# Context tokens' value sums on VectorE instead of TensorE, and a second PSUM buffer for the experts' first products

## The chip, the cores and the metric

The kernel runs on one core of a Trainium2 chip. The core has five engines with instruction queues of their own: TensorE (matrix products into PSUM), VectorE and ScalarE (element-wise work), GpSimd (here mostly the issue of gathers from memory) and SyncE (the issue of the other transfers). In the profile they are PE, DVE, ACT, POOL and SP. The metric is the device time of one execution in microseconds. Each engine works through its instructions in the order of the program and waits at an instruction until its operands and its output buffer are free.

## What is computed

A two-layer network over 512 latent tokens and 256 context tokens of width 1024: layer 0 is a gated DeltaNet, layer 1 attention, each followed by a mixer of experts (PEER). The mixer is what the change touches. For every token and each of 8 heads it picks 16 of 16384 experts by their scores; an expert is a row of the table u and a row of the table v:

```python
def block_fn(xb):
    ...
    idx = jnp.take_along_axis(cand_i, pos, axis=-1)          # 8 heads x 16 picks a token
    gate = jax.nn.softmax(best_s, axis=-1)
    act = jax.nn.gelu(jnp.einsum('pd,phkd->phk', xb, u_tab[idx]).astype(jnp.float32), approximate=False)
    coef = (gate * act).astype(xb.dtype)
    return jnp.einsum('phk,phkd->pd', coef, v_tab[idx])
```

The last line is the sum in question: for a token, 128 rows of v, each times a coefficient. Context tokens need the mixer in layer 0 only, since after layer 1's attention has read them nothing else does.

## The kernel before

Tokens are worked on in blocks of 128: latents 0 to 3, context 0 and 1. A mixer's tokens go one of two ways. Latents 0 to 2 (ND = 3) are evaluated *densely*: all 16384 experts in 128 blocks of 128, with a matrix of gates that is zero where an expert was not picked. Latent block 3 and, in layer 0, both context blocks are *gathered*: only the picked rows of u and v are read, with indirect transfers that GpSimd issues, 128 rows of 4 KB (one tile `row`) each.

In layer 0 the stages around the change follow one another like this: the DeltaNet; `routing` of the latents (the score products `qp` and the best 16 of each half, then the picks by block); `gates_build` (for each token two one-hot tiles A and B on VectorE and their product `gp` on TensorE); `dense` (for each of 128 blocks of experts the first products `up`, a Gelu into `c`, times the gates, and the second products `y` with the rows of v); then `attention`, which begins with a norm of each latent block and the projections `pa`. `act` computes `up` and the Gelu of one block; about half of the blocks are computed ahead, during `routing` and `gates_build` (`tock`), and their `c` is kept in memory. `up` has one PSUM bank, `y` has six.

The gathers are a background queue (`bg`) of generators. At fixed places in the loops `tick` adds a number from the table RATE to a credit and takes one step of the first generator for each whole credit; `drain(keep)` takes all steps at once until `keep` generators are left. A step issues one gather into one of four buffers `row` (GB = 4) and the instruction that uses it:

- `gather_u`: a scalar_tensor_tensor on VectorE that multiplies the rows by the tokens' values and sums along the row (L967).
- `gather_vt`, for latent block 3: partition t holds token t, step k gathers the k-th pick of all 128 tokens, and one scalar_tensor_tensor on VectorE (L984) adds row times coefficient to `y`; for block 3 the profile names this `lhs`.
- `gather_v`, for the context: a step gathers the 128 picks of one token. The sum over picks is a product on TensorE, `yp` (L1020): two calls of 512 columns, each with a 128x32 tile of `Cz` whose only nonzero column holds the token's coefficients. A call becomes two records in the trace. It works by halves of 64 tokens.

Three of the four context halves (NVA = 3) are queued ahead of the latents' gathers, the fourth behind them; it is left in the queue by `drain(2 * NX - NVA)` and taken within the attention's projections by their ticks and by the `drain()` ahead of the context's own norm, which reads its result. The order in which the attention takes latent blocks is 3, 1, 2, 0.

The instruction order on each engine is not the order in which the code is written. A scheduler (`schedule_with_timeline_sim=True`) reorders instructions while it builds the program; gathers and the VectorE instructions that use them keep their order among each other. Once built, the order is fixed.

Of the kernel before, what the change touches and what calls it, by code (L numbers as in the profile page):

```python
# [18 lines left out]
P = 128  # L19
# [12 lines left out]
AHEAD = [i for r in (0, 2, 1, 3) for i in range(r, PK, 4)]      # blocks of experts, in the order of their evaluation ahead  # L32


class Kern:
# [18 lines left out]
    # gathers are issued in small steps between the other work  # L54
# [67 lines left out]
    def ada(self, l, r, pool=None):  # L122
        """chunks 2 * r and 2 * r + 1 of a layer's modulations, for latents (row 0) and context (row 1)"""
# [24 lines left out]
    def mod_rows(self, pool, l, s, sub, norm, nb=1, pool_g=None, **kw):  # L148
        """A = norm_g*(1+scale), S = shift, as rows on all partitions"""
        nc = self.nc  # L150
        A = pool.tile([P, D], F32, name="modA", bufs=nb)
        S = pool.tile([P, D], F32, name="modS", bufs=nb)
        g = (pool_g or pool).tile([P, D], F32, name="modg", **kw)
        nc.sync.dma_start(g, self.I[norm][l:l + 1, :].to_broadcast([P, D]))
        self.ada_row(S, l, s, 3 * sub)
        self.ada_row(A, l, s, 3 * sub + 1)
        nc.vector.scalar_tensor_tensor(A, A, 1.0, g, op0=ALU.add, op1=ALU.mult)
        return A, S

    def norm_mod(self, pool, x, A, S, h):  # L160
        """h <- rmsnorm(x) * A + S"""
# [8 lines left out]
    def transp_split(self, pp, tag, h, hi, lo, b):  # L170
        """h [128, 1024] -> hi/lo[:, kb, b*128:...]"""
# [10 lines left out]
    # tokens on the free axis: 0..511 latents, 512..767 context  # L182
    def gate_math(self, p, pp, gx, n, G):
# [23 lines left out]
        # log1p(e) = ln(u) * e / (u - 1), or e where u rounds to 1  # L207
# [30 lines left out]
    def dn_in(self, G, later, ast, rec):  # L238
        """q, k, v, z and the gates; rec's first step is traced before the last heads, beside which it runs"""
# [67 lines left out]
    def dn_qkv(self, G, p, pp, pwp, hi, lo, wtile, heads, nb):  # L307
# [4 lines left out]
        W2 = TL + 4 + TC          # conv output span: latents, gap of 4, context  # L312
        XC = TL + 6               # start of the context in the padded row
# [83 lines left out]
    def dn_z(self, p, pp):  # L397
        """2 * silu(z)^T of the latents"""
# [24 lines left out]
    def dn_rec(self, seq, G, og_d, st_d):  # L423
# [5 lines left out]
        with ExitStack() as st:  # L429
# [8 lines left out]
            for g0 in range(0, QH, GR):  # L438
                pks, Pss, Us = [], [], []
                pg = p if g0 // GR % 2 else pq  # L440
                for hh in range(GR):
                    h = g0 + hh
                    Ps = pg.tile([P, MH, 2, P], F32, name="Pm", bufs=GR)
                    U = pg.tile([P, MH, 2, P], F32, name="U", bufs=GR)     # (c, v), dir
# [5 lines left out]
                    for c in range(n):  # L450
# [4 lines left out]
                        km = pq.tile([P, 2, 2, P], F32, name="km", bufs=2)     # (kk, kq), dir  # L455
                        nc.vector.tensor_mul(km, kk.unsqueeze(2).to_broadcast([P, 2, 2, P]), self.tri.unsqueeze(1).to_broadcast([P, 2, 2, P]))
                        rp = pqp.tile([P, 2, 2, P], F32, name="rp")
                        ar = pq.tile([P, 2, 2, P], F32, name="ar", bufs=2)     # (v, dir)
# [116 lines left out]
    def dn_inv(self, p, pp, Us, MH, Z64):  # L575
        """Us[head][:, m, dir] <- (I + U)^-1, U triangular (upper for dir 0, lower for dir 1)."""
# [23 lines left out]
        R1 = t4("R1", [P, 2 * M, 32])     # rows of the inverses' transposes  # L600
        R2 = t4("R2", [P, 2 * M, 32])     # rows of the inverses
# [9 lines left out]
        # (source, target) blocks  # L611
# [56 lines left out]
    def dn_out(self, seq, og_d, xin, xout, put):  # L668
        """xout[b] = xin[b] + g1 * (o @ w_out); put(b, rows) for every finished block"""
# [33 lines left out]
    def attention(self, xl, xc, order, rows, A0, gst, ost, pst):  # L703
        """(softmax(q k^T) v)^T of the latents, split, by heads; context is read after the gathers that finish it"""
# [134 lines left out]
    def attention_out(self, xl, xout, put):  # L839
        """xout[b] = xl[b] + g1 * (o @ w_out); put(b, rows) for every finished block"""  # L840
# [21 lines left out]
    def routing(self, l, hi, lo, T, gate, idx, order, done=None):  # L862
        """gate[b], idx[b]: [128 tokens, 8 heads, 16]"""
        nc, I = self.nc, self.I
        n = T // P
        with self.tc.tile_pool(name="rt", bufs=1) as q, self.tc.tile_pool(name="rtp", bufs=1, space=PS) as pp:
# [32 lines left out]
            for b in order:  # L899
# [29 lines left out]
                # places are STEP apart, so that the picked candidate's is the smallest difference  # L929
                nc.vector.tensor_add(ci, ci, iota.unsqueeze(1).to_broadcast([P, PH, NC_]))  # L930
                # the first eight picks lie in the staircase of eight
# [25 lines left out]
    def gather_u(self, l, p, hs, gate, idx, coef):  # L957
        """coef[t, (head, pick)] = gate * gelu(<u_pick, h_t>)"""
# [14 lines left out]
    def gather_vt(self, p, y, coef, idx, g2row, xin, put):  # L973
        """put(xin + g2 * sum over picks of coef * v_pick), by 128 tokens"""
# [20 lines left out]
    def gather_v(self, p, pv, pp, Cz, coef, idx, g2row, xin, xout, s):  # L995
        """xout = xin + g2 * sum over picks of coef * v_pick, by 64 tokens: partitions are (32 tokens, half row, token)"""
        nc = self.nc
        sl = lambda q: slice(32 * q, 32 * q + 32)
        hv = lambda q: slice(512 * (q % 2), 512 * (q % 2) + 512)
        l, r, m = g2row  # L1000
        ixf = pv.tile([P, P], F32, name="ixf")
        nc.vector.tensor_copy(ixf, idx.rearrange("p h k -> p (h k)"))
        yp = pp.tile([P, 512], F32, name="yp")
        nc.tensor.transpose(yp[:, 0:P], coef, self.ident)
        nc.tensor.transpose(yp[:, P:2 * P], ixf, self.ident)
        iT = pv.tile([P, P], I32, name="iT")
        nc.vector.tensor_copy(iT, yp[:, P:2 * P])
        cT = pv.tile([P, P], F32, name="cT")
        nc.vector.tensor_copy(cT, yp[:, 0:P])
        Cd = Cz.rearrange("p (g q) -> p g q", g=2)[:, :, 0:32 * 32:33]  # L1010
        nc.vector.tensor_copy(Cd, cT[:, 64 * s:64 * s + 64].rearrange("p (g i) -> p g i", g=2))
        yp = pp.tile([P, 512], F32, name="yp")
        for i in range(32):
            for g in range(2):
                t = 64 * s + 32 * g + i
                v = p.tile([P, D], F32, name="row", tag="row", bufs=self.gbufs)
                nc.gpsimd.indirect_dma_start(out=v, out_offset=None, in_=self.I["peer_v"],  # L1017
                                             in_offset=bass.IndirectOffsetOnAxis(ap=iT[:, t:t + 1], axis=0))
                for j in range(2):
                    nc.tensor.matmul(yp[sl(2 * g + j), :], Cz[:, (32 * g + i) * 32:(32 * g + i + 1) * 32], v[:, j * 512:(j + 1) * 512],  # L1020
                                     start=i == 0, stop=i == 31)
                if (i, g) == (28, 0):
                    fin = p.tile([P, D], F32, name="row", tag="row", bufs=self.gbufs)
                    xt, yt = fin[:, 0:512], fin[:, 512:D]
                    for q in range(4):
                        nc.sync.dma_start(xt[sl(q)], xin[64 * s + 32 * (q // 2):64 * s + 32 * (q // 2) + 32, hv(q)])
                        c0 = (m % 2) * D + 512 * (q % 2)
                        nc.sync.dma_start(yt[sl(q)], self.ada_d[l][m // 2][r:r + 1, c0:c0 + 512].to_broadcast([32, 512]))
                yield
        nc.vector.tensor_mul(yt, yt, yp)  # L1030
        nc.vector.tensor_add(yt, yt, xt)
        for q in range(4):
            nc.sync.dma_start(xout[64 * s + 32 * (q // 2):64 * s + 32 * (q // 2) + 32, hv(q)], yt[sl(q)])

    def gates_build(self, l, tbs, gate, idx, G_d, pk):
        """G_d[64-token group][j, i, t]: gate of expert i * 128 + j for every token; the last group is returned, in SBUF"""
# [201 lines left out]
def body(ctx, tc, I, out, dbg=None, upto=99):  # L1238
# [74 lines left out]
    for i in range(NVA):  # L1313
        vctx(i // 2, i % 2)
# [128 lines left out]
```

## Time and profile before

| | |
|---|---|
| time, median of three runs | 4883.66 us (4878.91 to 4895.90) |
| span of the profiled execution | 4891.1 us |
| TensorE busy | 4329.9 us, 89% |
| VectorE busy | 3587.0 us, 73% |
| ScalarE busy | 1866.5 us, 38% |
| GpSimd busy | 1321.5 us, 27% |
| memory traffic | 245 GB/s on average |

The profiled execution has no device time beside its span; the span is 7.4 us above the median and within the three runs. A row of a group reads: line of the code, engine, operation, output<-inputs, shapes, count, then busy time and mean length of one, then the idle time of the engine just ahead of these instructions and what ended it. In a row of stages the first figures are start and end in microseconds from the span's start. TensorE's records of successive products overlap, since they are pipelined; the distance of their starts is what one costs. VectorE's overlap a little as well.

### The profile page before, as it was taken

What the parts mean: (1) busy time and instruction counts of PE and PEld (TensorE: products, weight loads), DVE (VectorE), ACT (ScalarE), POOL (GpSimd) and SP (SyncE); (2) the same over time, 40 slices, a digit from 0 to 9 for tenths busy, and PEclk for the clock granted to TensorE, in tenths of its full rate; (3) what the DMA queues carried; (4) which work ended last, traced back from release to release, by engine and by line L of the source; (5) the groups of instructions that cost most, each with busy time, mean ns of one, the idle gap of its engine ahead of it and who ended that gap; (6) DMA issues with size and microseconds to landing.
All of it is one profiled execution on the core that took longest, in us unless ns stands there. A gap on an engine that the chain in (4) does not pass through costs nothing. (4 is left out here: it accounts for less than half of the span.)

```text
span 4891.1 us, 68996 instructions
## 1 busy us (share of the span) xinstructions
PE 4329.9 (89%) x24564; PEld 3455.1 (71%) x24564; DVE 3587.0 (73%) x8483; ACT 1866.5 (38%) x3605; POOL 1321.5 (27%) x1111
## 2 busy tenths in 40 slices
PE   6999669757569698999999999988997999999998
PEld 3778547545444556666788888745687998888887
DVE  4667825899965857566688888645579888888886
ACT  2335553447450213344333333223333554333333
POOL 0000000134344433222333334440000102444441
PEclk8999789768679899999999999999999999999999
DMA  7744246447578877777999999872133678999996
GB/s 296 261 150 135 75 144 191 153 148 254 177 242 317 301 240 268 269 260 272 329 349 351 339 339 337 292 268 74 61 112 107 215 260 287 355 334 335 336 324 230
DMA packets 480616, 1196.55 MB, mean 245 GB/s; under 512 B 40752, under 2 KB 239152, under 8 KB 470416
## 3 DMA queue, kind: packets, MB, share of 16 engines
q1 hardware_dynamic: 332816, 655.21, 38.2%
q0 software_dynamic: 147456, 536.94, 31.5%
q8 instruction: 194, 3.18, 0.3%
q14 instruction: 150, 1.23, 0.1%
HBM read 1079.50 MB, written 112.49 MB: 244 GB/s over the span
## 5 line engine op out<-in xcount | busy, mean ns | idle before, releaser
L965 POOL DMA_INDIRECT row<-in_peer_u,idx x512 | 613.2, 1198 | 1513.3 <-DVE row L967 706.3
L100 PE MATMUL up<-hil,uh 128*128 128x384 f32 x2048 | 709.4, 346 | 44.7 <-ACT c L1094 44.1
L102 PE MATMUL up<-hil,ul 128*128 128x384 f32 x2048 | 697.2, 340 | 0.0
L101 PE MATMUL up<-lol,uh 128*128 128x384 f32 x2048 | 696.1, 340 | 0.0
L100 PE MATMUL y<-vh,ch 128*128 128x512 f32 x1536 | 602.8, 393 | 9.1 <-ACT ch L106 7.6
L101 PE MATMUL y<-vl,ch 128*128 128x512 f32 x1536 | 602.9, 393 | 0.0
L102 PE MATMUL y<-vh,cl 128*128 128x512 f32 x1536 | 508.8, 391 | 0.0
L981 POOL DMA_INDIRECT row<-in_peer_v,idx x256 | 339.9, 1328 | 456.3 <-DVE lhs L984 374.5
L100 PEld LDWEIGHTS up<-hil,uh 128*128 128x128 f32 x2048 | 386.9, 189 | 94.8 <-ACT c L1094 65.4
L106 ACT CAST uh<-ur 128x1024 fp32r<-128x1024 f32 x256 | 268.3, 1048 | 454.3 <-PE up L101 322.3
L1017 POOL DMA_INDIRECT row<-in_peer_v,iT x256 | 279.5, 1092 | 557.7 <-PE yp L1020 473.7
L107 DVE TENSOR_TENSOR vl<-vr,vh 128x1024 fp32r<-128x1024 f32 x256 | 312.9, 1224 | 127.1 <-ACT vh L106 125.1
L106 ACT CAST vh<-vr 128x1024 fp32r<-128x1024 f32 x256 | 268.6, 1051 | 359.9 <-PE y L102 325.0
L101 PEld LDWEIGHTS up<-lol,uh 128*128 128x128 f32 x2048 | 387.1, 189 | 19.2 <-issue 10.9
L102 PEld LDWEIGHTS up<-hil,ul 128*128 128x128 f32 x2048 | 386.5, 189 | 18.2 <-issue 15.1
L107 DVE TENSOR_TENSOR ul<-ur,uh 128x1024 fp32r<-128x1024 f32 x256 | 312.1, 1220 | 74.7 <-ACT uh L106 70.1
L967 DVE SCALAR_TENSOR_TENSOR row<-row,ghs 128x1024 f32<-128x1024 f32 x256 | 311.2, 1222 | 73.7 <-DMA row<-in_peer_u,idx 72.7
L1066 DVE TENSOR_SCALAR A<-iotar,kt 128x128 f32<-128x128 f32 x768 | 221.8, 289 | 174.4 <-PE gp L1068 171.9
L100 PEld LDWEIGHTS y<-vh,ch 128*128 128x128 f32 x1536 | 289.8, 189 | 70.3 <-ACT ch L106 9.1
L102 PEld LDWEIGHTS y<-vh,cl 128*128 128x128 f32 x1536 | 288.6, 188 | 64.6 <-issue 4.2
L984 DVE SCALAR_TENSOR_TENSOR lhs<-row,lcf,lhs 128x1024 f32<-128x1024 f32 x254 | 325.1, 1280 | 9.6 <-DMA row<-in_peer_v,idx 8.0
L101 PEld LDWEIGHTS y<-vl,ch 128*128 128x128 f32 x1536 | 290.1, 189 | 56.3 <-issue 2.5
(397 smaller groups left out, 8788.1 us busy)
## 6 DMA issues: line engine op xcount, KB each, us to landing
ur<-in_uT SPq DMA_DIRECT2D x256, 512.0 KB
vr<-in_peer_v SPq DMA_DIRECT2D x256, 512.0 KB
w<-in_ada_w SPq DMA_DIRECT2D x48, 1024.0 KB
G_d<-st SPq DMA_DIRECT2D x10, 4096.0 KB
gt<-G_d SPq DMA_DIRECT2D x64, 640.0 KB
act_d<-c SPq DMA_DIRECT2D x129, 192.0 KB
c<-act_d SPq DMA_DIRECT2D x129, 192.0 KB
wr<-in_dn_w_in SPq DMA_DIRECT2D x48, 512.0 KB
```

Of the source, the lines that this page charges most:

```text
L100: first = mm(ps, lh, rh, start=start, stop=False)
L101: mm(ps, lh, rl, start=False, stop=False)
L102: mm(ps, ll, rh, start=False, stop=stop)
L106: self.nc.scalar.copy(hi, src)
L107: self.nc.vector.tensor_sub(lo, src, hi)
L965: nc.gpsimd.indirect_dma_start(out=u, out_offset=None, in_=self.I["peer_u"], in_offset=bass.IndirectOffsetOnAxis(ap=ix[:, k:k + 1], axis=0))
L967: mv = nc.vector.scalar_tensor_tensor(u, u, 1.0, hs, op0=ALU.mult, op1=ALU.mult, accum_out=coef[:, k:k + 1])
L981: nc.gpsimd.indirect_dma_start(out=v, out_offset=None, in_=self.I["peer_v"], in_offset=bass.IndirectOffsetOnAxis(ap=ix[:, k:k + 1], axis=0))
L984: keep(nc.vector.scalar_tensor_tensor(y, v, coef[:, k:k + 1], y, op0=ALU.mult, op1=ALU.add))
L1017: nc.gpsimd.indirect_dma_start(out=v, out_offset=None, in_=self.I["peer_v"], in_offset=bass.IndirectOffsetOnAxis(ap=iT[:, t:t + 1], axis=0))
L1066: nc.vector.tensor_scalar(A, iota, kt[:, 0, t:t + 1], None, op0=ALU.is_equal)
```

## The change

Both context blocks now use `gather_vt` like latent block 3: 128 steps a block, each a gather of one pick of 128 tokens and a multiply-add on VectorE into the block's own tile `ghs`. `gather_v`, its tables `Cz`, index transposes and PSUM bank are gone. The two context blocks are queued ahead of everything else, and `drain()` ahead of the attention empties the queue. The PSUM bank that came free becomes a second buffer of `up`, in both layers. Three numbers of layer 0's RATE differ: steps per score product in `routing` 5 to 3, per head in the picks 3 to 2.5, per group of four tokens in `gates_build` 0.88 to 1.2. The file also loses its comments; line numbers from 996 on are 40 lower.

```diff
-    def gather_v(self, p, pv, pp, Cz, coef, idx, g2row, xin, xout, s):
...
-        for i in range(32):
-            for g in range(2):
-                t = 64 * s + 32 * g + i
-                v = p.tile([P, D], F32, name="row", tag="row", bufs=self.gbufs)
-                nc.gpsimd.indirect_dma_start(out=v, out_offset=None, in_=self.I["peer_v"],
-                                             in_offset=bass.IndirectOffsetOnAxis(ap=iT[:, t:t + 1], axis=0))
-                for j in range(2):
-                    nc.tensor.matmul(yp[sl(2 * g + j), :], Cz[:, (32 * g + i) * 32:(32 * g + i + 1) * 32], v[:, j * 512:(j + 1) * 512],
-                                     start=i == 0, stop=i == 31)
...
-        ps = self.upp.tile([P, 512], F32, name="up")[:, :T]
+        ps = self.upp.tile([P, 512], F32, name="up", bufs=2)[:, :T]
...
-RATE = ([1.0, 3.3, 5.0, 3.0, 0.88, 2.6, 3.15, 2.6, 0.6, 3, 0.08], [0, 0, 0, 0, 0.27, 2.6, 0, 1.32, 6.25, 0, 0])
+RATE = ([1.0, 3.3, 3.0, 2.5, 1.2, 2.6, 3.15, 2.6, 0.6, 3, 0.08], [0, 0, 0, 0, 0.27, 2.6, 0, 1.32, 6.25, 0, 0])
...
-    gat.open_v(gst)
     k.dense_open(lst, 0, ND, hi, lo)
-    vctx = lambda b, s: gat.v_half(b, idx[1, b], (0, 1, 5), rows(xm_c, b), rows(xo_c, b), s)
-    for i in range(NVA):
-        vctx(i // 2, i % 2)
+    for b in range(NX):
+        gat.v(b, idx[1, b], (0, 1, 5), rows(xm_c, b), lambda y, b=b: nc.sync.dma_start(rows(xo_c, b), y))
...
-    for i in range(NVA, 2 * NX):
-        vctx(i // 2, i % 2)
...
-    k.drain(2 * NX - NVA)
+    k.drain()
```

What the scheduler makes of it is seen in the order of the instructions. First GpSimd's queue of gathers in layer 0, as the difference from before (idx_91 and idx_92 are the context blocks' picks, idx_90 latent block 3's):

```order
-L965 DMA row<-in_peer_u,idx_92 128x1024 x27
-L1017 DMA row<-in_peer_v,iT 128x1024 x192
+L965 DMA row<-in_peer_u,idx_92 128x1024 x29
+L981 DMA row<-in_peer_v,idx_91 128x1024 x128
+L981 DMA row<-in_peer_v,idx_92 128x1024 x128
 L965 DMA row<-in_peer_u,idx_90 128x1024 x128
 L981 DMA row<-in_peer_v,idx_90 128x1024 x128
-L1017 DMA row<-in_peer_v,iT 128x1024 x22
```

The gathers of the fourth half, of which the first 22 stand here, moved from behind the latents' gathers to ahead of them; the number of gathers is the same.

Second, VectorE near the start of `gates_build` of layer 0, before:

```order
L1066 TENSOR_SCALAR A<-iotar,kt 128x128
L1067 TENSOR_SCALAR B<-iotar,kt 128x128
L107 TENSOR_TENSOR ul<-ur,uh 128x1024
L1066 TENSOR_SCALAR A<-iotar,kt 128x128
L1067 TENSOR_SCALAR B<-iotar,kt 128x128
```

and now (`ghs` is a context block's sum):

```order
L1026 TENSOR_SCALAR A<-iotar,kt 128x128
L984 SCALAR_TENSOR_TENSOR ghs_6340<-row,gcf_6341,ghs_6340 128x1024
L1027 TENSOR_SCALAR B<-iotar,kt 128x128
L107 TENSOR_TENSOR ul<-ur,uh 128x1024
L1026 TENSOR_SCALAR A<-iotar,kt 128x128
L984 SCALAR_TENSOR_TENSOR ghs_6340<-row,gcf_6341,ghs_6340 128x1024
L1027 TENSOR_SCALAR B<-iotar,kt 128x128
```

The multiply-adds of gathered tiles stand between the one-hot tiles, where there were none.

Third, VectorE from the end of `dense` of layer 0 to the first norm of the attention, before (`rt_` is a finished block of the dense tokens, `hrow` the first tile of the attention):

```order
L1156 TENSOR_TENSOR rt__27332<-rt__27332,rx 128x512
L1155 TENSOR_TENSOR rt__27340<-y_20100,dg_27328 128x512
L1156 TENSOR_TENSOR rt__27340<-rt__27340,rx 128x512 x2
L88 TENSOR_SCALAR nm_ss<-nm_ss 128x1
L1155 TENSOR_TENSOR rt__27348<-y_20101,dg_27328 128x512
L1155 TENSOR_TENSOR rt__27348<-y_20102,dg_27328 128x512
L88 TENSOR_SCALAR nm_ss<-nm_ss 128x1
L1156 TENSOR_TENSOR rt__27348<-rt__27348,rx 128x512 x2
L166 SCALAR_TENSOR_TENSOR hrow<-lhs_12955,nm_ss,modA 128x1024
L166 SCALAR_TENSOR_TENSOR hrow<-rt__27340,nm_ss,modA 128x1024
```

and now:

```order
L1115 TENSOR_TENSOR rt__26994<-y_19786,dg_26974 128x512
L1116 TENSOR_TENSOR rt__26994<-rt__26994,rx 128x512 x2
L984 SCALAR_TENSOR_TENSOR lhs_12955<-row,lcf_12956,lhs_12955 128x1024 x2
L157 SCALAR_TENSOR_TENSOR modA<-modA,modg 128x1024
L984 SCALAR_TENSOR_TENSOR lhs_12955<-row,lcf_12956,lhs_12955 128x1024 x95
L991 TENSOR_TENSOR lhs_12955<-lhs_12955,row 128x1024
L992 TENSOR_TENSOR lhs_12955<-lhs_12955,row 128x1024
L88 TENSOR_SCALAR nm_ss<-nm_ss 128x1
L166 SCALAR_TENSOR_TENSOR hrow<-lhs_12955,nm_ss,modA 128x1024
L88 TENSOR_SCALAR nm_ss<-nm_ss 128x1
L168 TENSOR_TENSOR hrow<-hrow,modS 128x1024
L166 SCALAR_TENSOR_TENSOR hrow<-rt__26986,nm_ss,modA 128x1024
```

Block 3's multiply-adds, which all stood ahead of `rt_` before, now reach from before `rt_` to the first norm; 102 of its 128 come behind the first `rt_`.

## Rows read from the trace of the kernel before

**Rows 1.** The page: span, busy time by engine, busy tenths of 40 slices

```profile
span 4891.1 us, 68996 instructions
...
PE 4329.9 (89%) x24564; PEld 3455.1 (71%) x24564; DVE 3587.0 (73%) x8483; ACT 1866.5 (38%) x3605; POOL 1321.5 (27%) x1111
...
PE   6999669757569698999999999988997999999998
...
DVE  4667825899965857566688888645579888888886
```

**Rows 2.** Nine stages: length, engines' busy us (instructions), granted clock, DMA share, GB/s

```profile
1645.50:1829.00 183.50, 180.15 (x838) 117.27 (x836) 126.43 (x597) 40.88 (x60) 73.84 (x67) 0.98 0.78 252
1829.00:1958.00 129.00, 111.70 (x575) 77.35 (x572) 102.31 (x400) 40.11 (x73) 52.47 (x41) 0.99 0.79 268
1958.00:2332.00 374.00, 351.74 (x1968) 246.57 (x1966) 226.75 (x816) 147.68 (x166) 101.97 (x100) 0.98 0.77 268
2332.00:3178.00 846.00, 844.41 (x4039) 724.94 (x4040) 668.91 (x969) 292.84 (x392) 327.56 (x279) 1.00 0.92 335
3178.00:3206.00 28.00, 16.30 (x74) 6.62 (x73) 20.91 (x30) 9.45 (x17) 14.26 (x14) 0.75 0.96 359
3206.00:3362.70 156.70, 134.16 (x566) 79.05 (x564) 64.42 (x168) 40.88 (x139) 52.27 (x54) 0.94 0.53 175
3567.00:3684.60 117.60, 115.79 (x592) 99.92 (x592) 98.48 (x547) 37.25 (x54) 0.00 (x0) 1.00 0.26 76
3684.60:3797.80 113.20, 83.23 (x424) 77.51 (x423) 100.20 (x395) 40.78 (x73) 0.00 (x0) 0.95 0.36 114
3797.80:4150.00 352.20, 340.72 (x2134) 330.07 (x2133) 301.84 (x936) 179.85 (x217) 54.96 (x45) 0.99 0.72 254
```

**Rows 3.** The same stages, instructions on yp alone (PE, PEld, DVE busy)

```profile
1645.50:1829.00 183.50, 47.83 (x184) 6.57 (x184) 0.00 (x0) 0.98 0.78 252
1829.00:1958.00 129.00, 34.57 (x162) 5.27 (x158) 1.18 (x3) 0.99 0.79 268
1958.00:2332.00 374.00, 106.76 (x402) 14.65 (x402) 1.17 (x3) 0.98 0.77 268
2332.00:3178.00 846.00, 22.47 (x86) 3.30 (x86) 1.17 (x3) 1.00 0.92 335
3206.00:3362.70 156.70, 37.14 (x164) 5.38 (x164) 0.69 (x1) 0.94 0.53 175
```

**Rows 4.** TensorE in order of time in the picks: start, length, instruction

```profile
1902.30 0.33 PE L100 MATMUL up<-hil,uh 128*128 128x384 f32 x1
1902.48 0.34 PE L101 MATMUL up<-lol,uh 128*128 128x384 f32 x1
1902.75 1.05 PE L1020 MATMUL yp<-row,Cz 128*32 128x512 f32 x4
1903.73 0.45 PE L102 MATMUL up<-hil,ul 128*128 128x384 f32 x1
```

**Rows 5.** The page's groups: busy, mean ns of one, idle time before them

```profile
L107 DVE TENSOR_TENSOR ul<-ur,uh 128x1024 fp32r<-128x1024 f32 x256 | 312.1, 1220 | 74.7 <-ACT uh L106 70.1
...
L984 DVE SCALAR_TENSOR_TENSOR lhs<-row,lcf,lhs 128x1024 f32<-128x1024 f32 x254 | 325.1, 1280 | 9.6 <-DMA row<-in_peer_v,idx 8.0
```

**Rows 6.** VectorE's groups in the gates

```profile
L1066 DVE TENSOR_SCALAR A<-iotar,kt 128x128 f32<-128x128 f32 x384 | 113.1, 295 | 136.3 <-PE gp L1068 135.8
```

**Rows 7.** A stretch with gathers alone: the window, then its DMA queue

```profile
1559.00:1590.40 31.40, 21.45 (x56) 9.57 (x55) 21.55 (x35) 1.07 (x2) 20.71 (x17) 0.90 0.81 274
...
q0 software_dynamic: 2361, 8.61, 81.0%
```

**Rows 8.** POOL's groups in dense

```profile
L981 POOL DMA_INDIRECT row<-in_peer_v,idx x128 | 156.1, 1220 | 229.8 <-DVE lhs L984 175.4 <-DVE c L1122 32.3 <-DMA row<-in_peer_v,idx 13.0
```

**Rows 9.** VectorE in order of time, the last step of block 3's sum

```profile
3129.95 1.22 DVE L992 TENSOR_TENSOR lhs<-lhs,row 128x1024 f32<-128x1024 f32 x1
```

**Rows 10.** TensorE's waits in layer 1's picks: us, times, longest

```profile
PE up L100 <- ACT c L1094: 30.0, 18, 2.9
```

More of the change, by code (lines that the diff above doesn't have):

```diff
@@ L993, in gather_vt @@
         put(y)
-    def gather_v(self, p, pv, pp, Cz, coef, idx, g2row, xin, xout, s):
[L997 to L1012, printed above, removed]
-        for i in range(32):
-            for g in range(2):
-                t = 64 * s + 32 * g + i
-                v = p.tile([P, D], F32, name="row", tag="row", bufs=self.gbufs)
-                nc.gpsimd.indirect_dma_start(out=v, out_offset=None, in_=self.I["peer_v"],
-                                             in_offset=bass.IndirectOffsetOnAxis(ap=iT[:, t:t + 1], axis=0))
-                for j in range(2):
-                    nc.tensor.matmul(yp[sl(2 * g + j), :], Cz[:, (32 * g + i) * 32:(32 * g + i + 1) * 32], v[:, j * 512:(j + 1) * 512],
-                                     start=i == 0, stop=i == 31)
[L1022 to L1033, printed above, removed]
     def gates_build(self, l, tbs, gate, idx, G_d, pk):
@@ L1170, in final @@
         return put
-RATE = ([1.0, 3.3, 5.0, 3.0, 0.88, 2.6, 3.15, 2.6, 0.6, 3, 0.08], [0, 0, 0, 0, 0.27, 2.6, 0, 1.32, 6.25, 0, 0])
+RATE = ([1.0, 3.3, 3.0, 2.5, 1.2, 2.6, 3.15, 2.6, 0.6, 3, 0.08], [0, 0, 0, 0, 0.27, 2.6, 0, 1.32, 6.25, 0, 0])
 URATE = ([0.44, 0.9, 0.07, 15], [0.23, 1.0, 0.33, 5])
 HA = 7
-NVA = 3
 AB = 6
@@ L1200, in rows @@
             self.coef.append(p.tile([P, P], F32, name=f"gcf{b}"))
-    def open_v(self, st):
-        k = self.k
-        self.pv = st.enter_context(k.tc.tile_pool(name="gav", bufs=1, side="right"))
-        self.pp = st.enter_context(k.tc.tile_pool(name="gavp", bufs=1, space=PS, side="right"))
-        self.Cz = self.pv.tile([P, 64 * 32], F32, name="Cz")
-        k.nc.gpsimd.memset(self.Cz, 0.0)
     def u(self, l, j, gate, idx):
@@ L1215, in v @@
         k.bg.append(k.gather_vt(self.p, self.hs[j], self.coef[j], idx, g2row, xin, put))
-    def v_half(self, j, idx, g2row, xin, xout, s):
-        k = self.k
-        k.bg.append(k.gather_v(self.p, self.pv, self.pp, self.Cz, self.coef[j], idx, g2row, xin, xout, s))
 class Rows:
```

## The prediction

> **What bounds the kernel now.** I read the page first. The core spans 4891.1 us; TensorE is busy 89% of it, VectorE 73% [rows 1]. The tenths show TensorE at 9 nearly everywhere from the 14th slice on, with VectorE at 8 in the dense stages, so a stage can be bound by either. I therefore cut the part that the change touches into stages (by the first and last instruction of each on VectorE and TensorE) and asked for the busy time of every engine in each [rows 2]. In the order of the rows: layer 0's latent routing (184 us), picks (129), gates (374), dense (846), a gap with the norms (28) and the attention's projections (157); then layer 1's routing, picks and gates (118, 113, 352).
>
> In the front of layer 0 (routing, picks and gates, 183.5 + 129 + 374 = 687 us) TensorE is busy 180 + 112 + 352 = 644 us and VectorE 126 + 102 + 227 = 455. TensorE binds it: in the gates VectorE sat idle 136 us for TensorE's gate products [rows 6]. Dense is TensorE alone, 844 of 846. The projections have TensorE busy 134 of 157.
>
> **What goes.** The one-column products `yp` held TensorE for 47.8 + 34.6 + 106.8 = 189 us of the front, 22.5 of dense and 37.1 of the projections [rows 3]. A gathered tile costs four of them, 0.98 us from the first to the next other product [rows 4], so 256 tiles are some 251 us, as the sums say.
>
> **What comes.** Each of 256 context tiles now needs one multiply-add on VectorE; the same instruction in the latents' gather takes 1.280 us [rows 5], so 256 x 1.28 = 328 us. The number of gathers (256 of 128 rows, 512 KB each) stays. So the work does not shrink, it changes engine, and what counts is in which stage VectorE meets it. That is fixed by the order in which VectorE's instructions are issued, which I counted stage by stage in both kernels (gathered rows' instructions; expert blocks' splits `ul`):
> - routing: 22 then 51 rows' instructions, 8 then 16 splits
> - picks: 0 then 44, 18 then 34
> - gates: 0 then 62, 31 then 7
> - dense: 256 then 275, 69 both
> - between the end of dense and the first attention norm: 0 then 102
>
> Before, the 64 tiles of the last half ran beside dense's end, the gap and the projections, on TensorE. Now all context tiles stand ahead of the latents' own gathers, and the latents' block 3 is what is late: 102 of its 128 sums come after dense's last results.
>
> **Front.** VectorE's busy time becomes, with 1.28 per sum and 1.22 per split [rows 2, 5]: routing 126 + 29 x 1.28 + 8 x 1.22 = 173; picks 102 + 44 x 1.28 + 16 x 1.22 = 178; gates 227 + 62 x 1.28 - 24 x 1.22 = 277. Together 628. TensorE keeps 644 - 189 = 455, as the splits only move between these stages. So VectorE binds the front. It cannot be under 628 (59 less than now); at the share that VectorE reaches in layer 1's gates, 302 of 352 or 0.86 [rows 2], it is 730 (43 more). TensorE bound that stage, so VectorE should do better here; I take the middle, 0.94, which is 668: **-19 us**.
>
> **Dense.** TensorE loses 22 of 844 us, VectorE goes from 669 to 669 + 19 x 1.28 = 693, still under 822, and the gathers stay as many (256 + 24 before, 275 now), so the DMA share of 0.92 does too. **-22 us**, between 0 (VectorE late for TensorE now and then) and -45.
>
> **The rows left over.** This is the term that decides. Ahead of the first norm of the attention, VectorE's order has 102 sums with nothing between the last 95. The norms of the three dense blocks stand behind them on the same engine, and TensorE's next instruction needs a norm. Nothing covers this: TensorE idles until the sums are through. Before, the block was finished at 3131 [rows 9], before dense ended. The pace is that of gathers alone, four buffers in turn. The trace has such a stretch, 31.4 us in which only gathers ran on the DMA queues: 8.61 MB at 274 GB/s, or 524288 B / 274 GB/s = 1.91 us for each 512 KB [rows 7]. Ends: VectorE's own 1.28 us, and the pace in dense, where 128 gathers of POOL took 156 + 230 = 386 us, 3.0 each [rows 8]. I take 1.91, as the row nearest to the case. Four rows are already in their buffers: 98 x 1.91 + 4 x 1.28 = 192, less 2 for what overlaps: **+190 us** (from 130 to 299). The chain behind it (scale, add, norm, transposes, first split) takes the place of the 28 us gap and is counted even.
>
> A page weighs in here. The Trainium skill, "DMA: Bandwidth & Descriptors", section on the anatomy of a DMA issued by GpSimd, gives about 2.0 us fixed plus size over 436 GB/s. As an estimate from that page a gather takes 3.2 us, with four in flight one lands every 1.2 us at best, faster than VectorE takes them, and this term would be 130. The stretch above disagrees (1.91), though it ran at 0.81 of the DMA engines' time and so was not at their limit.
>
> **Projections.** 157 us less the 37 of `yp` and some 8 of the 22 us in which TensorE is idle there, part of it behind the last context half: **-45 us**, between -37 and -60 (all idle time gone).
>
> **Layer 1.** The only edit there is the second PSUM buffer. In its picks TensorE waits 30 us in 18 pieces for the Gelu to free the one buffer [rows 10], and is busy 83 of 113. The order now has 27 blocks' splits in the picks (18 before) and 39 in the gates (48). With 24 products per block at about 0.175 us [rows 4], 4.2 us: picks TensorE 83 + 38 = 121, so about 124 us (+11); gates 341 - 38 = 303 for TensorE and 302 - 11 = 291 for VectorE, so about 318 (-34). **-23 us**, between 0 and -45.
>
> The transposes, the copies and the memset of the old gather (a few us in the front) are counted at nothing, and so is the work before 1645 us, whose order is the same up to them.
>
> **Sum.** -19 - 22 + 190 - 45 - 23 = +81 on the profiled span of 4891.1: 4972. The three timed runs have a median of 4883.7, 7 below that span, so 4965.
>
> **Rivals.**
> 1. *VectorE is never idle* (faster). Wherever gathers feed VectorE, a row is always there when it asks. Place: the front and the rows left over; price 1.28 us per row; it decides when the pace of the left-over rows falls below about 1.5 us with the front at 628 (the other terms give back 149 us). Then -59 - 22 + 130 - 45 - 23 = -19, which is 4865. For it: in the front a gather is wanted only every 4 us or so. Against it: in the gather-only stretch VectorE was busy only 21.6 of 31.4 us [rows 7]. By the page quoted above this is how the left-over rows would go.
> 2. *Both stages at their slow ends* through one cause, gathers that land as slowly as in dense. VectorE then waits in the front too: +43 - 22 + 299 - 45 - 23 = +252, or 5136. Against it: dense has 335 GB/s on the queues and its gathers were held back by VectorE's order, not by DMA.
> 3. *The second PSUM buffer does nothing* (the change doesn't do what it says there): layer 1 and dense at 0, so +81 + 45 = +126, 5010. For it: dense shows TensorE 844 of 846 busy with one buffer.
>
> **How the numbers follow.** The forecast gets 0.55, rival 3 0.12 (a variant inside its range), rival 2 0.13, rival 1 0.2. Faster or slower means by over 0.3%, about what a measurement of this kernel can tell: below 4869 or above 4898. Rival 1's cases lie from 4840 to 4905: 0.13 faster, 0.07 no change. To the forecast's lower tail I give 0.03 each of faster and no change. Faster 0.16, same 0.1, slower 0.74. The range from 4866 to 5060 leaves some 0.1 on each side.
>
> **What would show it.** Right: after dense a stretch of 150 to 230 us with TensorE nearly idle, POOL gathering and VectorE doing only sums at 1.9 us a row; the front at 640 to 700 us with VectorE over 0.9; no `yp`; layer 1's wait of TensorE for the Gelu gone. Wrong: the stretch is not there or under 120 us (the order does not bind, or rows come faster), or the front shortens by over 60 us, which VectorE's work would not allow.

## Result and profile after

The changed kernel takes 4941.4 us (median of 4 runs, 4938.5 to 4949.1), the kernel before 4888.6 beside it (the three runs of the table and one more): ratio 1.0118, 95% interval 1.0100 to 1.0137. It is slower by 1.2%; 4965 was forecast. The profiled execution took 4938.9 us with a span of 4937.1, 46.0 more than [rows 1].

The page after: span and instructions, each engine's busy time with its share of the span, and 40 equal slices with TensorE's busy tenths, VectorE's, and TensorE's granted clock.

```profile
span 4937.1 us, 67307 instructions
PE 4132.8 (84%) x23532; PEld 3478.3 (70%) x23532; DVE 3889.8 (79%) x8719; ACT 1874.2 (38%) x3605; POOL 1394.0 (28%) x1110
...
PE   6999669757568889878999999027999998999998
...
DVE  4667726899966899998888888675579889888886
...
PEclk8999789768679899868999999559999998999999
```

TensorE's busy time fell by 197 us and VectorE's grew by 303, in the directions of the move (the prediction counted 251 and 328), but the hole is new: slices 26 and 27 read 0 and 2 for TensorE, where [rows 1] has 9 and 8, and the granted clock there is 0.5.

The stages of [rows 2], cut at the same instructions: window, length, each engine's busy us (instructions), granted clock, DMA share, GB/s. In order: layer 0's latent routing, picks, gates, dense, the stretch from dense to the projections, projections; layer 1's routing, picks, gates.

```profile
1650.10:1819.80 169.70, 164.00 (x863) 148.37 (x863) 168.55 (x633) 52.62 (x76) 60.49 (x52) 0.99 0.82 258
1819.80:1991.80 172.00, 146.63 (x806) 142.83 (x805) 169.50 (x456) 62.99 (x104) 71.76 (x45) 0.94 0.82 274
1991.80:2263.10 271.30, 210.28 (x968) 179.37 (x966) 270.33 (x853) 115.06 (x119) 70.50 (x66) 0.73 0.69 242
2263.10:3085.20 822.10, 820.19 (x3960) 723.01 (x3960) 685.85 (x976) 289.87 (x391) 355.48 (x271) 1.00 0.94 339
3085.20:3305.70 220.50, 4.15 (x18) 3.14 (x16) 148.15 (x127) 5.03 (x9) 124.79 (x102) 0.51 0.81 273
3305.70:3429.00 123.30, 99.74 (x414) 76.69 (x413) 69.27 (x175) 45.31 (x147) 17.17 (x17) 0.91 0.17 50
3630.70:3746.10 115.40, 115.40 (x593) 100.19 (x592) 97.38 (x545) 37.63 (x53) 0.00 (x0) 1.00 0.27 80
3746.10:3861.60 115.50, 113.03 (x635) 110.60 (x634) 109.91 (x404) 53.27 (x91) 0.00 (x0) 1.00 0.52 166
3861.60:4159.30 297.70, 280.31 (x1750) 271.30 (x1748) 260.92 (x874) 161.42 (x183) 33.13 (x32) 0.95 0.67 232
```

Against before: front (the first three) 687 to 613, **-74**; dense 843 to 822, **-21**; dense to the projections 31 to 220.5, **+190**; projections 156 to 123, **-33**; layer 1's three stages 544 to 529, **-16**; the rest adds up to 0 (5 more before the routing, 5 less later). (Before is cut to the tenth here, so dense and the gap read 843 and 31 where [rows 2] have 846 and 28. Layer 1's three stages read 544 where [rows 2] add up to 583, because the last row of [rows 2] is not the gates alone: it runs 38 us into layer 1's dense, whose first `y` starts at 4112.1. The gates of layer 1 before, as a window:)

```profile
3797.80:4112.10 314.30, 302.87 (x1972) 298.22 (x1970) 269.50 (x883) 166.79 (x201) 37.97 (x32) 1.00 0.68 241
```

In the front, the third row has VectorE busy 270 of 271 us. What it waited for over the whole 613 us (us, times, longest), then what TensorE waited for, and VectorE's costliest group there:

```profile
DVE ghs L984 <- DMA row<-in_peer_v,idx: 1.7, 2, 1.3
DVE row L967 <- DMA row<-in_peer_u,idx: 1.2, 2, 0.6
...
PE gp L1028 <- DVE B L1027: 49.3, 51, 1.3
PE up L102 <- DVE ul L107: 20.2, 8, 14.4
```

```profile
L984 DVE SCALAR_TENSOR_TENSOR ghs<-row,gcf,ghs 128x1024 f32<-128x1024 f32 x136 | 173.4, 1275 | 1.7 <-DMA row<-in_peer_v,idx 1.7
```

The roles are exchanged: in [rows 6] VectorE waited 136 us for the gate products, and now it waits for almost nothing while TensorE waits for it.

The hole after dense: TensorE's instructions around it (start, length, idle time before them), then who waited for VectorE's last add of the late block (us, times), then the middle 190 us as a window, and VectorE's sums in it.

```profile
3084.03 1.52 PE L102 MATMUL y<-vh,cl 128*128 128x512 f32 x6
3300.30 1.94 PE L176 MATMUL tr<-ident,hrow 128*128 128x128 f32 x8 [214.74 <-issue]
```

```profile
  ACT hrow L164: 216.4, 1
```

```profile
3100.00:3290.00 190.00, 0.00 (x0) 0.00 (x0) 125.61 (x100) 0.00 (x0) 116.02 (x94) 0.50 0.83 277
```

```profile
L984 DVE SCALAR_TENSOR_TENSOR lhs<-row,lcf,lhs 128x1024 f32<-128x1024 f32 x96 | 123.3, 1285 | 61.6 <-DMA row<-in_peer_v,idx 60.1
```

TensorE's row says "issue" for 215 us, so nothing there names the cause; the row of who waited does: ScalarE's square of the first norm, L164, stood 216 us for the last add of the late block (L992). In between, 96 sums in 190 us are 1.98 us a row, four other instructions of VectorE included. VectorE is busy 126 of 190 and waits 60 for the next row.

### The profile page after: what moved, and what is told of

Same layout as the page of the kernel before. It is cut to its first block, busy times and chain, and to the rows that moved or that the text cites. A ratio compares the mean times of both kernels' runs of the same rounds, so it can differ in the third digit from the quotient of the medians.

```text
span 4937.1 us, 67307 instructions
## 1 busy us (share of the span) xinstructions
PE 4132.8 (84%) x23532; PEld 3478.3 (70%) x23532; DVE 3889.8 (79%) x8719; ACT 1874.2 (38%) x3605; POOL 1394.0 (28%) x1110
## 5 line engine op out<-in xcount | busy, mean ns | idle before, releaser
L965 POOL DMA_INDIRECT row<-in_peer_u,idx x512 | 630.7, 1232 | 1502.1 <-DVE row L967 694.4
L981 POOL DMA_INDIRECT row<-in_peer_v,idx x512 | 672.5, 1313 | 927.8 <-DVE lhs L984 280.5
L1028 PE MATMUL gp<-A,B 128*128 128x128 f32 x1536 | 324.4, 342 | 63.0 <-DVE B L1027 52.8
L1028 PEld LDWEIGHTS gp<-A,B 128*128 128x128 f32 x1536 | 280.8, 230 | 102.0 <-DVE B L1027 71.4
L984 DVE SCALAR_TENSOR_TENSOR ghs<-row,gcf,ghs 128x1024 f32<-128x1024 f32 x254 | 324.7, 1278 | 6.8 <-DMA row<-in_peer_v,idx 5.7
```

What stands on the lines that cost most here:

```text
L965: nc.gpsimd.indirect_dma_start(out=u, out_offset=None, in_=self.I["peer_u"], in_offset=bass.IndirectOffsetOnAxis(ap=ix[:, k:k + 1], axis=0))
L984: keep(nc.vector.scalar_tensor_tensor(y, v, coef[:, k:k + 1], y, op0=ALU.mult, op1=ALU.add))
L1028: nc.tensor.matmul(ps[:, j], B, A, start=True, stop=True)
```

## Experiments

Stages of each profiled execution (us; "to norm" is dense to the first product of the projections; layer 1 is its routing, picks and gates; rows late are sums left between dense and the projections, and sums beside the projections, by VectorE's order as issued, from which the traces differ by one or a few at the edges; \* is a context tile's sum on TensorE, counted in the trace):

| run | rows late | to routing | front | dense | to norm | projections | layer 1 | span |
|---|---|---|---|---|---|---|---|---|
| before | 10\*, 41\* | 1645.5 | 687 | 843 | 31 | 156 | 544 | 4891.1 |
| changed | 102, 0 | 1650.1 | 613 | 822 | 220.5 | 123 | 529 | 4937.1 |
| e1 | 2, 90 | 1650.2 | 627 | 825 | 30 | 218 | 528 | 4862.0 |
| e2 | 30, 0 | 1646.5 | 692 | 911 | 80 | 121 | 544 | 4973.2 |
| e3 | 94, 0 | 1646.2 | 632 | 826 | 205 | 123 | 542 | 4954.5 |
| e4 | 10\*, 41\* | 1650.4 | 683 | 843 | 30 | 155.5 | 530 | 4869.8 |
| e5 | 92, 0 | 1653.4 | 509 | 820 | 197 | 122 | 528.5 | 4811.8 |
| e6 | 40, 0 | 1625.4 | 620 | 848 | 92 | 122 | 530 | 4820.2 |
| e7 | 2, 12 | 1628.2 | 659.5 | 871 | 34.5 | 130 | 527 | 4829.4 |
| e8 | 102, 0 | 1654.7 | 616 | 820 | 222 | 124 | 527 | 4942.5 |
| e9 | 2, 38 | 1626.2 | 616 | 843 | 32.5 | 141 | 530 | 4768.3 |
| e10 | 0, 0 | 1629.2 | 665 | 899 | 21 | 124 | 545 | 4860.9 |
| e11 | 116, 0 | 1683.3 | 621 | 841 | 290 | 121 | 526.5 | 5061.6 |

**e1: context block 1 behind the latents.**

```
-    for b in range(NX):
-        gat.v(b, ...)
+    vctx(0)                       # ahead of the latents, as before
     k.routing(0, hi, lo, TL, *lat, order, gathers)
+    vctx(1)
-    k.drain()
+    k.drain(1)
```

> The changed kernel with context block 1 queued behind the latents' gathers instead of ahead of them (context sums stay on VectorE); the drain before the attention keeps one block back. By VectorE's order 2 sums instead of 102 stand between dense and the first attention norm, and 92 context rows stand beside the projections. Theory A (the loss is only the order of the queue): the 220 us after dense fall to about 30, and the projections grow from 123 us to about 92 x 1.95 = 180 to 190, so 4941 - 190 + 65 = 4816 us, range 4800 to 4850: faster than both kernels. Rival B (the move of the sums to VectorE is itself what costs): the rows only change place and hold the projections' own VectorE work (splits, norms) back just as long; 4920 to 4945. Rival C (the rows beside the projections are paced as in dense, 3 us each): 92 x 3 = 276, 4905.

Measured: 4861.6 us against 4881.5 for the kernel before beside it, ratio 0.996 (0.9943 to 0.9976). The sums are still on VectorE and the kernel is now faster than both, so the move of the engine is not what made it slower; rival B falls. The hole is gone (30 us), but the time is 12 us above the range of theory A: the projections took 218, not 180 to 190. By the trace 84 of the late sums stand there; the last ends at 3324, 2.3 us for each, and 26 us with that block's last adds, norm and products follow. The projections' window, then VectorE's and TensorE's longest waits in it:

```profile
3131.70:3349.90 218.20, 108.95 (x412) 81.54 (x412) 168.52 (x257) 44.38 (x143) 133.71 (x98) 0.75 0.71 233
```

```profile
DVE ghs L984 <- DMA row<-in_peer_v,idx: 26.7, 31, 2.5
...
PE tr L176 <- DVE hrow L168: 51.9, 2, 51.5
```

VectorE has work of its own there (69 us in the changed kernel), with 107.7 us of sums on top; TensorE stands 52 us at the end for the norm of the last context block. The front is 14 longer: by the trace 21 of the latents' dot products moved into it.

**e2: sums on TensorE, all of the context ahead of the latents.** From the kernel before:

```
-NVA = 3
+NVA = 4
-    k.drain(2 * NX - NVA)
+    k.drain()
```

> The kernel before (context sums stay one-column products on TensorE) with the fourth half of the context's blocks queued ahead of the latents too, so that no gather is left beside the projections and all is drained before the attention. 30 of the latents' sums now stand after dense instead of none. Theory A (order): the gap of 31 us becomes 31 + 26 x 1.95 + 4 x 1.28 = about 85 to 90, the projections fall from 156 to about 123, dense takes some 40 more of TensorE's context tiles at 0.98 us: 4889 + 56 - 33 + 39 = 4950, range 4915 to 4965: slower by the order alone, with no sum moved to VectorE. Rival B (the order matters little, the engine does): within 0.5% of 4889.

Measured: 4976.2 us, ratio to before 1.0191 (1.0172 to 1.0210). No sum moved to another engine, and the order alone makes the kernel before slower than the change does. The time is 11 us above the range of theory A. To the norm 80 us and projections 121 are near what was expected (85 to 90, and 123); dense grew by 68, not 39, and is the larger part of the loss. TensorE's busy time on `yp` there went from 22 [rows 3] to 75, which is 53 of it; the other 15 are not settled. The stretch to the norm as a window: 49 us more than before for some 30 sums, 1.6 each.

```profile
3249.80:3330.20 80.40, 3.93 (x17) 3.16 (x17) 55.72 (x56) 5.09 (x10) 33.34 (x30) 0.51 0.79 283
```

**e3: one PSUM buffer again; e4: the second buffer alone.** From the changed kernel, and from the kernel before:

```
-  name="up", bufs=2)
+  name="up", bufs=1)

-  name="up")
+  name="up", bufs=1 + l)
```

> The changed kernel with one PSUM buffer for the dense first products, as before; all else as changed. Layer 1's picks hold 18 blocks' splits and its gates 48 again. Theory A (the buffer is worth what layer 1 shows, 17 us, and nothing where VectorE binds the front): 4941 + 17 = 4958, and up to 15 less where 94 instead of 102 rows are left after dense; range 4940 to 4962. Rival (the buffer is also what lets layer 0's front run 74 us shorter): 4985 or more. Rival (the buffer does nothing): 4930.

> The kernel before with the second PSUM buffer for layer 1's dense first products alone (layer 0's PSUM has no room for it there). Layer 1's picks hold 27 blocks' splits (18) and its gates 39 (48). Theory A: layer 1 shortens by 17 us as between the two kernels: 4871, ratio 0.9965. Rival (what was gained in layer 1 came with something else of the change, such as where the work starts): 4889, ratio 1.000.

Measured: e3 4959.8 us, 18 above the changed kernel; e4 4870.5, ratio to before 0.9977 (0.9967 to 0.9987). The total of e3 is as expected, but two terms in it were not: the front is 19 longer (expected 0), and that and layer 1's 13 are partly given back by 16 less after dense. So the second buffer also shortens layer 0's front, by 19 of the 74 us. e4 shortens layer 1 by 15, so the buffer is the whole gain there. TensorE's wait for the Gelu in layer 1's picks, in e3 and then in e4 and in the changed kernel (which read alike):

```profile
PE up L100 <- ACT c L1054: 30.1, 18, 3.0
```

```profile
PE up L100 <- ACT c L1094: 1.0, 1, 1.0
```

The 30.0 us of [rows 10] come back with one buffer and go with two. In layer 0's front of e3 TensorE waits for the Gelu too, and VectorE for ScalarE's half of a split, where the changed kernel has 10.9 and 0.8 us:

```profile
PE up L100 <- ACT c L1054: 56.4, 42, 2.8
DVE ul L107 <- ACT uh L106: 12.9, 10, 3.9
```

**e5: narrow context sums.**

```
-  nc.vector.scalar_tensor_tensor(y, v, coef[:, k:k + 1], y, ...)
+  nc.vector.scalar_tensor_tensor(y[:, :w], v[:, :w], coef[:, k:k + 1], y[:, :w], ...)   # context: w = 64
```

> The changed kernel with the context rows' multiply-adds (all but each block's first pick) on 64 of the 1024 columns: 960 columns of the context tokens' sums are left out; gathers, order and all else stay (92 instead of 102 latent sums are left after dense). Theory A (VectorE binds layer 0's front, which is busy 100% there for hundreds of us): 145 rows of the front lose about 1.1 us each, up to 160 us, until TensorE binds, busy 521 of its 613 us: front 530 to 560 instead of 613. Rival B (TensorE or the gathers bind the front): it stays at 600 to 613. Both expect dense at 815 to 825, since it is not VectorE's, and 92 left-over rows at 1.95 us, some 205 from dense to the projections.

Measured (one execution): 4813.5 us. The front fell from 613 to 509, further than expected. A narrow sum takes 0.27 us, so 147 of them return up to 148 us; 104 came out. The three windows of the front:

```profile
1653.40:1792.00 138.60, 135.18 (x705) 120.73 (x704) 134.39 (x632) 42.88 (x63) 65.84 (x58) 0.99 0.90 301
1792.00:1916.80 124.80, 118.56 (x654) 115.66 (x653) 118.17 (x446) 54.43 (x92) 59.17 (x41) 0.97 0.94 329
1916.80:2162.60 245.80, 224.40 (x1279) 193.57 (x1277) 225.99 (x874) 132.96 (x145) 76.61 (x73) 0.97 0.89 323
```

VectorE did bind the front, and rival B falls. TensorE and VectorE are now each busy 478 to 479 of 509 us and the DMA share is 0.9, so what would bind next is not told apart here. TensorE's busy time fell below the 521 us that theory A took for its limit, with as many instructions (2638, and 2633 in the changed kernel): the granted clock of the front is 0.97 instead of 0.86. Dense and the 197 us after it stay, as both theories said.

**e6: five gather buffers; e11: three.**

```
-ZT = 8, 4          (e6 only: room)
+ZT = 8, 3
-GB = 4
+GB = 5             (e11: 3)
```

> The changed kernel with five gather buffers instead of four (room made by 3 instead of 4 buffers of the early z work). VectorE's order leaves 40 sums after dense instead of 102, so 329 rows instead of 275 stand in dense. Theory A (a row alone costs 1.95 us for the time that a gather takes, with four in flight): the pace falls to 4/5, 1.56 us, and the 220 us after dense become 28 + 35 x 1.56 + 5 x 1.28 = 90. Rival B (the DMA engines set the pace, 0.8 of their time taken): 1.9 us still, 28 + 35 x 1.9 + 6 = 100. For dense both: the 54 rows more are 28 MB on top of 823 us x 337 GB/s = 277 MB; at 350 GB/s, the most seen, 872 us instead of 821 if transfers bind there, 821 if TensorE still does. In all 4941 - 125 + (0 to 50) = 4815 to 4865.

> The changed kernel with three gather buffers instead of four; 116 sums instead of 102 are left after dense by VectorE's order. Measured so far: 1.93 us for each row left over with four buffers, some 1.65 with five. Theory A (a gather takes a fixed time of some 7.7 us from issue to landing and use, so the pace is that time over the number of buffers): 2.57 us, the stretch from dense to the projections 28 + 114 x 2.57 = 320 us. Rival B (the DMA engines set the pace): 28 + 114 x 1.93 = 250 us. Dense 820 under both, the front up to 20 us longer where VectorE now waits for rows; the whole 4941 + 100 = 5040 or 4941 + 30 = 4970, and some 20 us more before the routing, as five buffers gave 25 there.

Measured: e6 4819.7 us, ratio to before 0.986 (0.9841 to 0.9879), so 1.4% faster than before and 2.5% faster than the change as made; e11 (one execution) 5063.4. Dense in e6 (its window), and e11's stretch of nothing but gathers with the sums in it:

```profile
2245.20:3093.60 848.40, 826.04 (x3956) 723.16 (x3957) 748.04 (x1031) 284.88 (x391) 445.31 (x327) 0.99 0.97 361
```

```profile
3160.00:3420.00 260.00, 0.00 (x0) 0.00 (x0) 146.78 (x118) 0.00 (x0) 117.04 (x110) 0.50 0.75 237
```

```profile
L984 DVE SCALAR_TENSOR_TENSOR lhs<-row,lcf,lhs 128x1024 f32<-128x1024 f32 x113 | 145.3, 1286 | 114.8 <-DMA row<-in_peer_v,idx 114.4
```

With three buffers a left-over row costs 260 / 113 = 2.30 us, with four 1.98, at DMA shares of 0.75 and 0.83. e11's stretch of 290 us lies between the 320 and 250 of its theories, and neither holds (the whole is above both, since dense took 841 instead of 820 and the work before the routing 33 us more): a gather's time is not fixed (3 x 2.30 = 6.9, 4 x 1.98 = 7.9), and the pace is not the DMA engines' alone. For five, (91.8 - 31) / 35 = 1.74 us is only an estimate from the stage's length. A window in it, and its sums:

```profile
3105.00:3170.00 65.00, 0.00 (x0) 0.00 (x0) 47.16 (x39) 0.00 (x0) 42.64 (x32) 0.50 0.92 328
```

```profile
L984 DVE SCALAR_TENSOR_TENSOR lhs<-row,lcf,lhs 128x1024 f32<-128x1024 f32 x34 | 43.7, 1285 | 15.8 <-DMA row<-in_peer_v,idx 15.2
```

These are 65 / 34 = 1.91 us a row with VectorE's other work in it, and (43.7 + 15.8) / 34 = 1.75 without (with four buffers, 1.98 and 1.93). Theory A's 1.56 was not reached, and the fifth buffer's gain in pace is small. The larger gain of the fifth buffer is another one: the order it brings puts 329 rows in dense instead of 275, and dense took 54 rows more for 26 us, at 361 GB/s instead of 339. Dense had room on the queues; four buffers left it unused.

**e7: e1 and e6 together.**

> Both at once: context block 1 behind the latents' gathers (as in the first experiment) and five gather buffers. By VectorE's order 332 rows stand in dense, 2 sums between dense and the norms, 12 rows beside the projections instead of 92. Theory A (rows are worth placing where TensorE works anyway): dense 821 to 875, gap 31, projections 218 down to 125 to 135; against the first experiment (4862) -90 + (0 to 50): 4770 to 4825, the fastest of all. Rival B (dense is already full on the DMA queues, 0.94): dense grows by 57 x 1.6 = 90 or more and nothing is won: 4860.

Measured: 4826.5 us, ratio to before 0.9877 (0.986 to 0.9893): 35 better than e1, just outside what A gave and no better than e6. Gap (34.5) and projections (130) are about as A said; dense grew by 46, and the gates by 32, because by the trace 43 of the latents' dot products (21 in e1) now stand in the gates, where VectorE is busy 305 of 318 us.

**e8: the numbers of RATE as before.**

```
-RATE = ([1.0, 3.3, 3.0, 2.5, 1.2, ...
+RATE = ([1.0, 3.3, 5.0, 3.0, 0.88, ...
```

> The changed kernel with the three numbers of the table RATE as before the change (5.0, 3.0, 0.88 instead of 3.0, 2.5, 1.2). VectorE's instructions stand in the same stages, row for row. Theory A (order as issued is all that the table could change): every stage within 3 us of the changed kernel, 4940. Rival B (the table sets the pace in another way): another front or another number of left-over rows.

Measured (one execution): 4944.3 us; every stage within 5 us of the changed kernel. The table has no part in the result that this run could show.

**e9: five buffers, and 40 picks of context block 1 late.**

```
     for b in range(NX):
         gat.v(b, ...)
+    last = k.bg.pop()
+    k.bg.append(islice(last, PH * TOPK - LATE))      # LATE = 40
     k.routing(0, hi, lo, TL, *lat, order, gathers)
+    k.bg.append(last)
-    k.drain()
+    k.drain(1)
```

> The changed kernel with five gather buffers, and the last 40 of context block 1's 128 picks queued behind the latents' gathers (the first 88 ahead). By VectorE's order 329 rows stand in dense, 2 sums between dense and the norms (40 with five buffers alone, 102 with the change) and 38 rows beside the projections. Theory A (rows between dense and the norms cost their full pace, rows beside the projections only what VectorE has no room for): against the run with five buffers alone (4820), the 94 us after dense fall to 31 and the projections grow from 122 to 145 to 160, as 92 rows made them 218: 4780 to 4795. Rival B (what is won in the gap is lost in the projections or the front, as with block 1 late as a whole, 4826): 4815 or more.

Measured: 4781.1 us, ratio to before 0.9781 (0.9764 to 0.9799): the fastest, 160 us under the change as made. Dense, the stretch to the norm, and the projections:

```profile
2242.50:3085.70 843.20, 824.04 (x3956) 722.20 (x3957) 747.82 (x1030) 286.72 (x391) 442.54 (x327) 1.00 0.98 364
3085.70:3118.20 32.50, 7.22 (x30) 5.14 (x28) 30.77 (x38) 8.51 (x16) 20.25 (x15) 0.57 0.97 365
3118.20:3259.60 141.40, 103.03 (x404) 77.17 (x404) 102.64 (x202) 42.60 (x141) 50.27 (x42) 0.84 0.48 155
```

Against e6, the 38 rows that moved make the projections 20 us longer (30 of them stand in that window by the trace) and the stretch to the norm 59 us shorter: 0.5 us a row in the new place, 1.6 in the old.

**e10: the kernel before with five buffers.**

```
-ZT = 8, 4
+ZT = 8, 3
-GB = 4
+GB = 5
-  name="gt", bufs=3)     name="wr", bufs=3)     name="qr", bufs=2)
+  name="gt", bufs=2)     name="wr", bufs=2)     name="qr", bufs=1)
```

> The kernel before (context sums on TensorE, same queue) with five gather buffers, room for which is made by one buffer less of the early z work, of the gates' tiles, of the projections' raw weights and of a rope tile. Theory A (the fifth buffer is worth most where rows are left over, which the kernel before has not): up to routing -25 us as in the run with five buffers on the changed kernel, the rest within 15 us: 4850 to 4880. Rival B (the fifth buffer speeds up any gather, so the changed kernel's gain by it says nothing of its left-over rows): -100 or more, 4785.

Measured: 4862.8 us, ratio to before 0.9959 (0.9943 to 0.9975), about 20 us. On the changed kernel the fifth buffer is worth 122: 129 won after dense and 25 before the routing, 26 and 7 lost in dense and the front. So its larger worth there is the left-over rows. The total here is as theory A said, its parts are not: all `yp` products came to stand before dense's end, so dense took 55 more, the projections 32 and the front 22 less. What the buffers given up for the fifth may cost is not shown by itself.

## Why the prediction was right, and where it was not

**Left-over rows, +190 forecast, +190 measured.** This step decided, and it was read from the right place: the order as issued has 102 sums ahead of the first norm, and the row price came from a stretch with gathers alone, 1.91 us [rows 7], where 1.98 was measured. e1 and e9 show it by removal on the same engine, e2 by adding it to the old one. That both numbers are 190 is partly luck: the sums run until 3292, 207 us after dense, with some 8 us of VectorE's other work among them, so they cost about 8 more than forecast, and the work around them, counted even at 31, about 8 less (14 us from the last sum to the first projection product). From the fixed time and the rate that the Trainium skill gives in "DMA: Bandwidth & Descriptors", section on the anatomy of a DMA issued by GpSimd, the prediction had an estimate of 1.2 us a row at best with four in flight; the trace disagrees with it (1.98).

**Front, -19 forecast, -74 measured.** The failed step is "at the share that VectorE reaches in layer 1's gates ... I take the middle, 0.94", and with it "It cannot be under 628". That VectorE binds was right (e5). But its share is 608 / 613 = 0.99, since it waits 2.9 us for rows in the whole front. The share of layer 1's gates belongs to a stage in which TensorE was the bound and VectorE waited for it; it said nothing of VectorE as the bound. (The stage was also cut wrong, 352 us for 314, but 270 / 314 is 0.86 as well; and the middle of 0.86 and 1 is 0.93, which gives -12.) The floor was 20 too high. Added one by one, the lengths of VectorE's instructions in the front grew by 170 us, from 580 to 751, as the forecast's 173 said; but beside other work the next instruction starts before one ends (3084.03 and 3085.24 for one of 1.29 us in VectorE's timeline), and with overlaps counted once its busy time grew by 153, from 456 to 608: 1.13 us for each of the 135 rows that came, not 1.28. Of the 55 us that the front was off, the floor is 21 and the share 34. The prediction also put the second buffer of `up` at nothing here without a reason: with one buffer the front is 632 and VectorE's share 614 / 632 = 0.97 (e3), so some 19 of the 34 are the buffer's. Rival 1's mechanism, a row always there when VectorE asks, is true of the front and false of the left-over rows, so its front (-59) came and its 130 did not. The prediction named "over 60 us" as a sign that it was wrong, and that sign came; the total still came within 24 us, since the projections and layer 1 gave back 19 of the 55.

**Dense, -22 against -21.** Right; TensorE binds it still, busy 820 of 822.

**Projections, -45 against -33.** The 37 us of `yp` went; the step "some 8 of the 22 us in which TensorE is idle there" failed. TensorE is idle 23.6 of 123.3 us now and 22.5 of 156.7 before. Before, it waited 5.9 us for context rows and 10.6 for VectorE's norms and rotations of the heads (6.2 + 4.4); now 14.8 for the latter (9.7 + 5.1). The waits (us, times, longest), before and now:

```profile
PE pa L100 <- DVE qn L761: 6.2, 2, 3.6
PE yp L1020 <- DMA row<-in_peer_v,iT: 5.9, 5, 2.2
PE tr L779 <- DVE qr L775: 4.4, 1, 4.4
```

```profile
PE pa L100 <- DVE qn L761: 9.7, 4, 5.3
PE tr L779 <- DVE qr L775: 5.1, 3, 4.4
```

**Layer 1, -23 against -16.** The mechanism was right (e3, e4: 13 and 15), its size off in two terms that partly cancel. The nine blocks that moved into the picks lengthened them by 2 instead of 11: TensorE's busy time there grew by 30 us, not 38, which is what it had idled. They shortened the gates by 17 (314 to 298) instead of 34: TensorE's busy time there fell by 23 (303 to 280), not 38, with the granted clock at 0.95 instead of 1.00.

**The sum.** -74 - 21 + 190 - 33 - 16 = +46 on the span; +81 was forecast. The front is 55 of the difference, and the projections and layer 1 give 19 of it back. Rival 3 (the buffer does nothing) falls by e3 and e4. Rival 2 (rows as slow as in dense) falls too: rows came at 1.98, not 3.0, and the front did not wait for them.

## What to carry to other kernels

When work moves from one engine to another, count where its instructions come to stand in the order, and look for the first instruction that needs the last of them: here the same 256 sums on the same engine made the kernel 1.2% slower or 2.2% faster by their place and one buffer. A background row was nearly free beside a stage that another engine binds (0.5 us in dense of e6 and beside the projections of e9) and cost its full transfer pace where only it was left (1.98). A share read from a stage bound by another engine is no estimate of what an engine reaches when it is the bound.

## Hardware seen in the runs that was not expected

- While TensorE stood idle after dense, its granted clock was 0.50 (1.2 GHz), and the first products of the projections took 0.80 us instead of 0.39 for the same shape; 3 us later they were at 0.39:

```profile
3305.75 0.80 PE L100 MATMUL pa<-wh,hi 128*128 128x512 f32 x1
3306.47 0.80 PE L101 MATMUL pa<-wl,hi 128*128 128x512 f32 x1
...
3308.84 0.39 PE L100 MATMUL pa<-wh,hi 128*128 128x512 f32 x1
```

- In the front's gates the granted clock is 0.73, with TensorE busy 210 of 271 us in pieces between waits for VectorE, and a gate product `gp` takes 385 ns there (290 before, at 0.98); in e5, where TensorE is busy 224 of 246, the clock is 0.97.
- By pace times buffers, a row kept its buffer longer when more were in flight: 6.9 us with three buffers and 7.9 with four, at 237 and 277 GB/s. Beside dense's own loads the queues moved 364 GB/s.
